# Stick-breaking sums of a two-layer transformer block: the long key rows in two float32r passes, and a place for block one's tables that is given back

## The chip, the core and the metric

The kernel runs on one core of a Trainium2 chip. The metric is device microseconds of one execution. The engines that matter are PE (TensorE, the matmuls), DVE (VectorE), ACT (ScalarE), POOL (GpSimd) and SP, which issues the DMAs. Each engine takes its instructions strictly in the order in which the program lists them, so an instruction that waits holds up all that stand behind it on its engine.

## What is computed

A first block (dilated and windowed attention and an MLP) is followed by two layers of a second block. Each of those layers has a gated feed-forward part, a mixer with three branches (stick-breaking attention, a gated matrix memory, latent attention) and another feed-forward part; there are 512 tokens of width 1024. The change is in the stick-breaking attention, four heads in each layer:

```python
def _stick_breaking_attention(q, k, v):
    """q,k,v: (B,H,S,d). A[t,s] = sigmoid(z_ts) * prod_{s<j<t} (1 - sigmoid(z_tj)), s < t. ..."""
    ...
        z = jnp.einsum('bhqd,bhkd->bhqk', qb, k[:, :, :n], preferred_element_type=jnp.float32) * scale
        ...
        log_keep = jnp.where(mask, jax.nn.log_sigmoid(-z), 0.0)
        ...
        within = jnp.einsum('bhqnj,js->bhqns', lk, tri_in)
        after = jnp.einsum('bhqm,mn->bhqn', jnp.sum(lk, axis=-1), _strict_lower(nk))
        later = (within + after[..., None]).reshape(b, h, Q_BLOCK, n)
        w = jnp.where(mask, jnp.exp(jax.nn.log_sigmoid(z) + later), 0.0)
```

For each query the weight of a key needs the sum of `log_keep` over all later keys up to the query. The sum within a block of 128 keys is a matmul with a triangular matrix; the sum over the later blocks is one row that is carried from block to block.

## The kernel before

**Weights.** `load_w` (L361) brings a weight tile by DMA into `wraw`, casts it on ACT to the upper part `whi` (float32r, L384) and subtracts on DVE to get the lower part `wlo` (L385). Nearly all matmuls are products in three float32r passes (`mm3`). There are two buffers for `wraw` and four each for `whi` and `wlo`: a DMA into `wraw` waits until the `wlo` subtraction of the tile two before it has read that buffer.

**Order.** The order on PE is written out by hand: jobs are generators, `Loom` gives each a due time when it yields a number, and inserts what is due between the weight matmuls; the yields of the stick-breaking heads are `T_SB`, `T_SBR` and `T_SBW` (L1682). On ACT, DVE, POOL and SP a scheduler sets the order when the program is built. `Slots` hands out SBUF places of 4096 bytes per partition (`ND` = 22 of them) and halves of these; a job that needs places yields a condition on `H.room`.

**Stick-breaking.** `sb_job` (L1155) takes the four heads of a layer in two pairs. `stick_scores` (L1428) makes the scores z transposed, keys on partitions, in four key blocks kb: block kb has 512 - 128 kb query columns, so kb 0 to 3 have 512, 384, 256 and 128. Two tiles hold them, one of 1024 columns (kb 0, 1, 3) and one of 256 (kb 2). `stick_head` (L1446) then works on one head: Abs, Exp and Ln on ACT (L1453 to L1455); `sp` and the new z on DVE (L1456, L1457); row 0 of each block is copied to `own` on ACT (L1464), and the diagonal 128 columns are masked on POOL (L1467). After `T_SB` come the four triangular matmuls `sbl<-sbp,trigt` in plain float32, kb 3, 2, 1, 0; between two of them a one-partition DVE add (L1477) puts the sum of the later blocks into row 0 of the next block. At the end DVE subtracts the sums from z (L1480), ACT takes the exponential (L1483), POOL masks the diagonals (L1486), and `sb_job` multiplies by v (`sbo`). The row add is

```python
V.tensor_add(self.tri(sp, kb - 1)[0:1, 128:n + 128], pl[kb][0:1, 0:n], own[kb])
```

**What runs beside it.** Between the stick-breaking steps of a layer's first pair PE multiplies weights (`pt`, six matmuls of 512 columns for one PSUM bank; the bank is read by DVE, `mlv`, L1594) and works on the latent attention (`mla_job`): four transposes `mT` for each head, read from PSUM by ACT into `mhT` (L1358); scores `mls`, reduced by DVE (L1382) and exponentiated by ACT (L1386); transposes `mlT` of the weights `mp`. `carry` and `carryT` are small transposes of the matrix memory's gates, with a chain of one-partition steps on DVE (L1520 to L1527). All these matmuls write one ring of eight PSUM banks, so a matmul also waits until what its bank held before has been read: in the changed program `carry` takes the bank of the first `mT` of the keys, and the first `sbl` of a pair takes the bank that the first `mlv` reads.

Of the kernel before, what the change touches and what calls it, by code (L numbers as in the profile page):

```python
# [155 lines left out]
class Net:  # L156
# [74 lines left out]
    def make_masks(self):  # L231
        nc, C = self.nc, self.const

        self.causal = C.tile([128, S], F32, name="causal")
        nc.vector.memset(self.causal, 0.0)
        own = self.causal[:, 384:512]
        self.sel(own, own, [[-1, 128]], 0, 1, ALU.is_ge, NEG)

        self.band = []
        for name, base in (("band0", 0), ("band1", -1)):  # L240
            m = C.tile([128, 256], F32, name=name)
            nc.vector.tensor_copy(m, self.causal[:, 256:512])
            self.sel(m[:, 0:128], m[:, 0:128], [[1, 128]], base, -1, ALU.is_ge, NEG)
            self.band.append(m)

        self.upper = C.tile([128, 128], F32, name="upper")
        self.sel(self.upper, self.ones, [[1, 128]], -1, -1, ALU.is_ge, 0.0)
        self.upper0 = C.tile([128, 128], F32, name="upper0")
        nc.vector.tensor_copy(self.upper0, self.upper)
        nc.vector.memset(self.upper0[0:1], 0.0)  # L250
        self.trigt = C.tile([128, 128], F32, name="trigt")
        self.sel(self.trigt, self.ones, [[-1, 128]], -1, 1, ALU.is_ge, 0.0)
        nc.vector.memset(self.trigt[0:1], 1.0)
        self.negup = C.tile([128, 128], F32, name="negup")
        nc.vector.memset(self.negup, 0.0)
        self.sel(self.negup, self.negup, [[1, 128]], 0, -1, ALU.is_ge, NEG)
        self.zrow = C.tile([16, 128], F32, name="zrow")
        nc.vector.memset(self.zrow, 0.0)
# [74 lines left out]
    def rope_table(self, name, src, goff, cos, sin, half):  # L333
# [2 lines left out]
        g = self.sc.tile([128, 2 * half], F32, name="rg" + name, tag="rg")  # L336
        nc.sync.dma_start(g, dram(src, goff, [[0, 128], [1, 2 * half]]))
        n = cos.shape[-1] // half
        A = C.tile([128, n, 2 * half], F32, name="rA" + name, tag="rA" + name)
        B = C.tile([128, n, 2 * half], F32, name="rB" + name, tag="rB" + name)  # L340
        cs = cos.rearrange("p (b f) -> p b f", f=half)
        sn = sin.rearrange("p (b f) -> p b f", f=half)
        gl = g[:, 0:half].unsqueeze(1).to_broadcast([128, n, half])
# [207 lines left out]
    def x_tok_job(self, out):  # L551
        for tb in range(TB):
# [212 lines left out]
    def block1(self):  # L765
# [41 lines left out]
        for b in range(TB):  # L807
# [3 lines left out]
        g2, *gains = self.columns("gains", [(a["ln2_g"][0], KB)] + [  # L811
            (a[k][l], KB) for l in range(2) for k in ("ffn1_norm_2", "mix_norm_2", "ffn2_norm_2")], 40.0)
        sinks = self.bcast_row(a["sinks"][0], 8, "sinks")
        self.make_rope()
        self.make_masks()

# [176 lines left out]
            nc.vector.tensor_mul(zt[m // 2][:, m % 2], pg, self.rrow)  # L993
        mix = [zt[i // 2][:, i % 2] for i in range(KB)]
        loom.wait(lambda: not any(left.values()), "units")
        M = T.tile([128, TB, 4], F32, name="dM", bufs=1)
        nc.vector.tensor_max(M, og[0][1][:, :, 0:4], og[1][1][:, :, 0:4])
        nc.vector.tensor_max(M, M, og[2][1][:, :, 0:4])
# [418 lines left out]


    def tri_tiles(self, name):
        return self.H.get(name, [128, 1024]), self.H.get(name + "2", [128, 256])  # L1420

    @staticmethod
    def tri(t, kb):
        o, n = {0: (0, 512), 1: (512, 384), 3: (896, 128), 2: (0, 256)}[kb]
        return t[1 if kb == 2 else 0][:, o:o + n]


    def stick_scores(self, q, k, pr, z):  # L1428

        nc, H = self.nc, self.H  # L1430
        yield lambda: H.room(4096, 4096, 1024, 1024)
        z += [self.tri_tiles("sbz") for _ in range(2)]
        for kbs, i, c0, c1 in ((1, 3), 0, 512, 1024), ((2,), 1, 0, 256), ((0,), 0, 0, 512):
            ps = [self.bank("sbs") for _ in range(2)]
            c = 0
            for kb in kbs:
# [9 lines left out]
    def stick_head(self, z):  # L1446

        nc, H = self.nc, self.H
        V, A, G = nc.vector, nc.scalar, nc.gpsimd
        yield lambda: H.room(4096, 4096, 1024, 1024)  # L1450
        t, sp = self.tri_tiles("sbt"), self.tri_tiles("sbp")
        for i in range(2):
            A.activation(t[i], z[i], AF.Abs)  # L1453
# [8 lines left out]
        for kb in (3, 2, 1, 0):  # L1462
            if kb:
                A.copy(own[kb], self.tri(sp, kb)[0:1])  # L1464
                G.memset(own[kb][:, 0:1], 0.0)
            d = self.tri(sp, kb)[:, 0:128]
            G.tensor_mul(d, d, self.upper0)  # L1467
        yield T_SB
        pl = {1: self.bank("sbl"), 2: self.bank("sbl")}
        pl[3] = pl[1][:, 384:512]  # L1470
        for kb in (3, 2, 1, 0):
            n = S - kb * 128
            if kb == 0:
                pl[0] = self.bank("sbl")
            self.mm(pl[kb][:, 0:n], self.trigt, self.tri(sp, kb), True, True)
            if kb:
                V.tensor_add(self.tri(sp, kb - 1)[0:1, 128:n + 128], pl[kb][0:1, 0:n], own[kb])  # L1477
                yield T_SBR
        for i, c0, c1, kb in ((0, 512, 1024, 1), (1, 0, 256, 2), (0, 0, 512, 0)):
            V.tensor_sub(z[i][:, c0:c1], z[i][:, c0:c1], pl[kb][:, 0:c1 - c0])  # L1480
        H.put(*sp)
        for i in range(2):
            A.activation(z[i], z[i], AF.Exp)  # L1483
        for kb in range(TB):
# [194 lines left out]

T_KD, T_HEADS, T_EXP, T_PT = 22.0, (13.0, 19.0), {1: 4.5, 2: 6.5}, 1.9  # L1680
T_MLA, T_MP, T_MPT = {"q": 12.0, "k": 5.0}, 6.0, 3.5
T_SB, T_SBR, T_SBW = 14.0, 2.5, 3.5  # L1682
T_MS, T_SILU = 3.0, 14.0
CREW = (2, 2, 2)
INS = ["x", "positions", "ln1_g", "w_in", "q_norm_a", "k_norm_a", "q_norm_b", "k_norm_b", "sinks", "w_branch_a",
# [25 lines left out]


ND, SCR = 22, 6
WB = (2, 4)
```

## Time and profile before

| | |
|---|---|
| median of 3 runs | 2324.08 us (2323.95 to 2324.93) |
| the profiled execution | 2323.26 us |
| its span in the profile | 2321.5 us |
| PE busy | 2306.3 us, 99% |
| DVE, ACT, POOL busy | 56%, 39%, 16% |
| the granted TensorE clock | 1.0 in every slice |

The profiled execution lasts 1.8 us longer than its span, so a change of the span is a change of the time. In the rows further down a PE row gives start and modelled duration; matmuls overlap, so what one costs is the distance to the start of the next. "x4" merges four instructions in a row.

### The profile page before, as it was taken

Reading aid. Unit: us, or ns where it says so; the run is one execution under the profiler, and the core shown is the slowest. Engines: PE = TensorE matmul, PEld = TensorE weight load, DVE = VectorE, ACT = ScalarE, POOL = GpSimd, SP = SyncE. Lnnn points to the kernel's source line nnn. Section 1 sums busy time; section 2 is a strip of 40 time slices with the busy share of each in tenths; the row PEclk is TensorE's granted clock in tenths of the full one; section 3 lists DMA queues with packets and bytes.
Section 4 is the critical chain, followed back from the end, with each engine's and each line's share of the span. In section 5 each row is a group of like instructions: output and inputs, shape, how many; then the busy total and the mean of one; then the engine's idle time right before and its main releaser. Section 6 shows DMA issues by size and latency. Waiting matters only on the chain.

```text
span 2321.5 us, 28445 instructions
## 1 busy us (share of the span) xinstructions
PE 2306.3 (99%) x10884; PEld 1902.3 (82%) x10884; DVE 1294.5 (56%) x2255; ACT 914.9 (39%) x1517; POOL 381.4 (16%) x385
## 2 busy tenths in 40 slices
PE   8999999999999999999999999999999999999999
PEld 7888888888888888877888888888888778888887
DVE  7844556444355445678564555455457674646552
ACT  7655432222223323656533333223236673333331
POOL 2000023101022112111111311211211101213110
PEclk9999999999999999999999999999999999999999
DMA  4223333233323323313323333333233142323332
GB/s 139 65 64 92 100 100 99 85 105 95 98 87 105 100 92 96 97 55 91 105 63 91 109 91 91 100 92 100 91 102 91 46 114 73 89 83 105 92 100 87
DMA packets 250525, 213.68 MB, mean 92 GB/s; under 512 B 14231, under 2 KB 234133, under 8 KB 250389
## 3 DMA queue, kind: packets, MB, share of 16 engines
q1 hardware_dynamic: 250388, 211.87, 30.8%
q8 instruction: 85, 1.39, 0.2%
q14 instruction: 52, 0.42, 0.1%
HBM read 208.64 MB, written 3.19 MB: 91 GB/s over the span
## 4 chain that ended last, share of the span: by engine, by line
PE 96%; ACT 1%; DVE 1%; DMA 1%; SPq 0%; issue 0%; ACTq 0%
PE pgate L205 15%; PE pd L205 15%; PE pt L205 13%; PE pg L205 10%; PE pa L205 10%; PE pu L205 8%; PE pf L205 6%; PE po L205 6%; PE pbr L205 5%; PE mls L205 1%; PE mnum L205 1%; PE sbl L205 1%; PE mss L205 1%; PE dio L205 1%; PE s L205 1%; PE pT L212 0%
## 5 line engine op out<-in xcount | busy, mean ns | idle before, releaser
L385 DVE TENSOR_TENSOR wlo<-wraw,whi 128x1024 fp32r<-128x1024 f32 (+3 forms) x394 | 550.6, 1398 | 412.3 <-ACT whi L384 407.4
L384 ACT CAST whi<-wraw 128x1024 fp32r<-128x1024 f32 (+3 forms) x394 | 404.6, 1027 | 649.7 <-PE pg L205 141.6
L205 PE MATMUL pd<-hidh,whi 128*128 128x512 f32 x520 | 202.3, 389 | 0.0
L205 PE MATMUL pd<-hidl,whi 128*128 128x512 f32 x520 | 202.3, 389 | 0.0
L205 PE MATMUL pd<-hidh,wlo 128*128 128x512 f32 x520 | 202.3, 389 | 0.0
L205 PE MATMUL pgate<-xh,whi 128*128 128x512 f32 x512 | 201.3, 393 | 0.0
L205 PE MATMUL pgate<-xh,wlo 128*128 128x512 f32 x512 | 199.4, 389 | 0.0
L205 PE MATMUL pgate<-xl,whi 128*128 128x512 f32 x512 | 199.2, 389 | 0.0
L205 PE MATMUL pt<-whi,xl 128*128 128x512 f32 (+2 forms) x480 | 172.1, 358 | 0.0
L205 PE MATMUL pt<-whi,xh 128*128 128x512 f32 (+2 forms) x384 | 140.4, 366 | 0.1
L205 PE MATMUL pa<-xl,whi 128*128 128x512 f32 x352 | 137.2, 390 | 0.8 <-DVE xl L476 0.7
L205 PE MATMUL pa<-xh,whi 128*128 128x512 f32 x352 | 137.6, 391 | 0.0
L205 PE MATMUL pg<-xh,whi 128*128 128x512 f32 x352 | 137.4, 390 | 0.0
L205 PE MATMUL pa<-xh,wlo 128*128 128x512 f32 x352 | 137.1, 389 | 0.0
L205 PE MATMUL pg<-xh,wlo 128*128 128x512 f32 x352 | 137.0, 389 | 0.0
L205 PE MATMUL pg<-xl,whi 128*128 128x512 f32 x352 | 137.0, 389 | 0.0
L205 PE MATMUL pt<-wlo,xh 128*128 128x512 f32 (+2 forms) x384 | 134.1, 349 | 0.0
L587 POOL TENSOR_TENSOR t<-t,t 128x512 f32<-128x512 f32 x44 | 56.8, 1290 | 426.6 <-ACT whi L384 313.4
L205 PEld LDWEIGHTS pd<-hidl,whi 128*128 128x128 f32 x520 | 97.6, 188 | 20.4
L205 PEld LDWEIGHTS pd<-hidh,whi 128*128 128x128 f32 x520 | 97.6, 188 | 20.3
L205 PEld LDWEIGHTS pd<-hidh,wlo 128*128 128x128 f32 x520 | 97.6, 188 | 20.1
L205 PEld LDWEIGHTS pt<-whi,xl 128*128 128x128 f32 x480 | 102.5, 214 | 12.6
(524 smaller groups left out, 4674.0 us busy)
## 6 DMA issues: line engine op xcount, KB each, us to landing
wraw<-in_w_in_dram SPq DMA_DIRECT2D x116, 512.0 KB
wraw<-in_ffn_wi_dram SPq DMA_DIRECT2D x176, 256.0 KB
wraw<-in_ffn_wo_dram SPq DMA_DIRECT2D x34, 512.0 KB
wraw<-in_w_up_dram SPq DMA_DIRECT2D x32, 512.0 KB
wraw<-in_w_out_dram SPq DMA_DIRECT2D x24, 512.0 KB
wraw<-in_w_down_dram SPq DMA_DIRECT2D x24, 512.0 KB
wraw<-in_w_in_dram SPq DMA_DIRECT2D x32, 256.0 KB
wraw<-in_ffn_wo_dram SPq DMA_DIRECT2D x12, 384.0 KB
```

Source lines behind the costliest of these rows:

```text
L205: self.nc.tensor.matmul(out, lhsT, rhs, start=start, stop=stop)
L384: nc.scalar.copy(hi, raw)
L385: nc.vector.tensor_sub(lo, raw, hi.bitcast(F32))
L587: nc.gpsimd.tensor_mul(t2, t2, t1)
```

## The change

The matmuls of kb 1 and kb 0 take their input in two float32r parts: `split_to` casts the 896 columns of both blocks on ACT into `sph` and subtracts on DVE into `spl`, and `trigr`, the triangular matrix as float32r, multiplies both into one bank. kb 3 and kb 2 stay in plain float32 and share a tile of 384 columns. The row that is carried into kb 1 and kb 0 is now added into `own`, and `row_split` puts its upper and lower parts into row 0 of `sph` and `spl` (a cast and a subtraction on DVE, on one partition). The scores come in the order (2, 3), 1, 0. The band masks and the rope tables of block one move into a `Slots` place `k1` that is put back after block one; `ND` becomes 23, and the conditions for places grow. The core of the diff:

```diff
-            m = C.tile([128, 256], F32, name=name)
+            m = self.k1[:, len(self.band) * 256:len(self.band) * 256 + 256]
...
-        self.trigt = C.tile([128, 128], F32, name="trigt")
-        self.sel(self.trigt, self.ones, [[-1, 128]], -1, 1, ALU.is_ge, 0.0)
-        nc.vector.memset(self.trigt[0:1], 1.0)
+        tri = self.scr("tri")[:, 0:128]
+        self.sel(tri, self.ones, [[-1, 128]], -1, 1, ALU.is_ge, 0.0)
+        nc.vector.memset(tri[0:1], 1.0)
+        self.trigr = C.tile([128, 128], F32R, name="trigr")
+        nc.vector.tensor_copy(self.trigr, tri)
+        self.trigt = self.trigr.bitcast(F32)
...
+    def row_split(self, hi, lo, t):
+        V = self.nc.vector
+        V.tensor_copy(hi, t)
+        V.tensor_sub(lo, t, hi.bitcast(F32))
...
+        self.k1 = H.get("k1", [128, 1024])
...
+        H.put(self.k1)
...
-        return self.H.get(name, [128, 1024]), self.H.get(name + "2", [128, 256])
+        return self.H.get(name, [128, 896]), self.H.get(name + "2", [128, 384])
 
     @staticmethod
     def tri(t, kb):
-        o, n = {0: (0, 512), 1: (512, 384), 3: (896, 128), 2: (0, 256)}[kb]
-        return t[1 if kb == 2 else 0][:, o:o + n]
+        i, o, n = ((0, 0, 512), (0, 512, 384), (1, 0, 256), (0, 896, 128) if t[0].shape[1] == 1024 else (1, 256, 128))[kb]
+        return t[i][:, o:o + n]
...
-        yield lambda: H.room(4096, 4096, 1024, 1024)
+        yield lambda: H.room(4096, 4096, 1536, 1536)
         z += [self.tri_tiles("sbz") for _ in range(2)]
-        for kbs, i, c0, c1 in ((1, 3), 0, 512, 1024), ((2,), 1, 0, 256), ((0,), 0, 0, 512):
+        for kbs, i, c0, c1 in ((2, 3), 1, 0, 384), ((1,), 0, 512, 896), ((0,), 0, 0, 512):
...
-        yield lambda: H.room(4096, 4096, 1024, 1024)
+        yield lambda: H.room(4096, 4096, 4096, 1536, 1536)
...
+        two = [H.get(n, [128, 896], F32R) for n in ("sph", "spl")]
+        self.split_to(*two, sp[0])
+        H.put(sp[0])
         yield T_SB
-        pl = {1: self.bank("sbl"), 2: self.bank("sbl")}
-        pl[3] = pl[1][:, 384:512]
+        pl = {2: self.bank("sbl")}
+        pl[3] = pl[2][:, 256:384]
         for kb in (3, 2, 1, 0):
             n = S - kb * 128
-            if kb == 0:
-                pl[0] = self.bank("sbl")
-            self.mm(pl[kb][:, 0:n], self.trigt, self.tri(sp, kb), True, True)
-            if kb:
-                V.tensor_add(self.tri(sp, kb - 1)[0:1, 128:n + 128], pl[kb][0:1, 0:n], own[kb])
-                yield T_SBR
-        for i, c0, c1, kb in ((0, 512, 1024, 1), (1, 0, 256, 2), (0, 0, 512, 0)):
+            if kb < 2:
+                pl[kb] = self.bank("sbl")
+                for i in range(2):
+                    self.mm(pl[kb][:, 0:n], self.trigr, self.tri(two[i:], kb), i == 0, i == 1)
+            else:
+                self.mm(pl[kb][:, 0:n], self.trigt, self.tri(sp, kb), True, True)
+            if kb == 3:
+                V.tensor_add(self.tri(sp, 2)[0:1, 128:n + 128], pl[kb][0:1, 0:n], own[kb])
+                yield T_SBR[0]
+            elif kb:
+                V.tensor_add(own[kb], pl[kb][0:1, 0:n], own[kb])
+                self.row_split(*(self.tri(two[i:], kb - 1)[0:1, 128:n + 128] for i in range(2)), own[kb])
+                yield T_SBR[1]
+        for i, c0, c1, kb in ((1, 0, 384, 2), (0, 512, 896, 1), (0, 0, 512, 0)):
             V.tensor_sub(z[i][:, c0:c1], z[i][:, c0:c1], pl[kb][:, 0:c1 - c0])
-        H.put(*sp)
+        H.put(sp[1], *two)
...
-T_SB, T_SBR, T_SBW = 14.0, 2.5, 3.5
+T_SB, T_SBR, T_SBW = 14.0, (2.5, 3.2), 3.5
...
-ND, SCR = 22, 6
+ND, SCR = 23, 6
```

On PE the rows stand as before except for the first parts of the stick-breaking work: in a layer's first pair all four `mls` of 128 columns now stand ahead of the two `sbl` of 128, two `mlT` stand between the `sbl` of the two heads' kb 1, and the four `mls` of 256 columns stand ahead of the `sbl` of kb 0 instead of behind it. In the second pair the `sbl` steps are spread further apart. On ACT and DVE more has moved. The places below are in the first layer's first pair; the second layer has the same order.

On ACT, around the copies of the latent attention's key transposes (`mhT<-mT,hgk`), before:

```order
L1455 ACTIVATE sbt2_7885<-sbt2_7885 128x256
L1358 ACTIVATE mhT_7969<-mT_7970,hgk_7148 96x512
L1464 COPY own_7922<-sbp_7910 1x128
L1464 COPY own_7923<-sbp_7910 1x384
L1464 COPY own_7922<-sbp2_7911 1x256
L1358 ACTIVATE mhT_7969<-mT_7982,hgk_7148 96x512
L384 CAST whi_8139<-wraw_8138 128x1024
L1358 ACTIVATE mhT_8000<-mT_8001,hgk_7148 96x512
L384 CAST whi_8312<-wraw_8311 128x1024
L1358 ACTIVATE mhT_8000<-mT_8013,hgk_7148 96x512
L384 CAST whi_8399<-wraw_8398 128x1024
```

and after, where `sph_7917` and `sph_7946` are the casts of the two heads:

```order
L1479 COPY own_7934<-sbp2_7923 1x256
L576 CAST sph_7917<-sbp_7894 128x896
L1479 COPY own_7935<-sbp_7922 1x384
L1373 ACTIVATE mhT_7974<-mT_7975,hgk_7145 96x512
L576 CAST sph_7946<-sbp_7922 128x896
L1373 ACTIVATE mhT_7974<-mT_7987,hgk_7145 96x512
L1373 ACTIVATE mhT_8005<-mT_8006,hgk_7145 96x512
L391 CAST whi_8276<-wraw_8275 128x1024
L1373 ACTIVATE mhT_8005<-mT_8018,hgk_7145 96x512
L391 CAST whi_8416<-wraw_8415 128x1024
```

The first head's cast now stands ahead of all four `mhT` copies and the second head's ahead of the last three; before, the first `mhT` copy came right behind the last Ln.

On DVE, ahead of the gate chain (`carry`), before:

```order
L1457 SCALAR_TENSOR_TENSOR sbz_7808<-sbz_7808,sbt_7909 128x1024
L1457 SCALAR_TENSOR_TENSOR sbz2_7807<-sbz2_7807,sbt2_7885 128x256
L385 TENSOR_TENSOR wlo_8140<-wraw_8138,whi_8139 128x1024
L1520 COPY carry_8022<-carry_8019 1x16
L1521 COPY carry_8022<-carry_8019 1x16
L1526 TENSOR_TENSOR carry_8022<-carry_8022 1x12
L385 TENSOR_TENSOR wlo_8313<-wraw_8311,whi_8312 128x1024
```

and after:

```order
L1472 SCALAR_TENSOR_TENSOR sbz_7805<-sbz_7805,sbt_7921 128x896
L577 TENSOR_TENSOR spl_7918<-sbp_7894,sph_7917 128x896
L392 TENSOR_TENSOR wlo_8147<-wraw_8145,whi_8146 128x1024
L577 TENSOR_TENSOR spl_7947<-sbp_7922,sph_7946 128x896
L1546 COPY carry_8027<-carry_8024 1x16
L1547 COPY carry_8027<-carry_8024 1x16
L1552 TENSOR_TENSOR carry_8027<-carry_8027 1x12
L392 TENSOR_TENSOR wlo_8277<-wraw_8275,whi_8276 128x1024
```

The two subtractions `spl` stand on both sides of the first `wlo`. Further along on DVE, at the first copy of a `pt` bank (`mlv`), before:

```order
L1524 TENSOR_TENSOR carry_8022<-carry_8022 1x4
L1525 TENSOR_TENSOR carry_8022<-carry_8022 1x4
L1594 SCALAR_TENSOR_TENSOR mlv_7791<-pt_7799,rcy_7216,br_mv_7789 128x4x128
L1382 ISA mp_8061,mlm_8062<-mls_8064,causal_440 128x128
L1382 ISA mlm_8062 128x1
L1382 ISA mp_8061,mlm_8062<-mls_8070,causal_440 128x128
```

and after:

```order
L1550 TENSOR_TENSOR carry_8027<-carry_8027 1x4
L1551 TENSOR_TENSOR carry_8027<-carry_8027 1x4
L392 TENSOR_TENSOR wlo_8417<-wraw_8415,whi_8416 128x1024
L1620 SCALAR_TENSOR_TENSOR mlv_7788<-pt_7796,rcy_7213,br_mv_7786 128x4x128
L1397 ISA mp_8066,mlm_8067<-mls_8069,causal_437 128x128
L1397 ISA mlm_8067 128x1
```

A third weight subtraction, `wlo_8417`, now stands ahead of `mlv` and of the reductions of the scores; before, it stood behind them all.

On ACT at the end of the pair, where `sbz` are the exponentials of the heads and `ysb` copies the product with v, before:

```order
L1483 ACTIVATE sbz_7806<-sbz_7806 128x1024
L1483 ACTIVATE sbz_7808<-sbz_7808 128x1024
L1386 ACTIVATE mp_8061,mld_8211<-mp_8061,mnm_8215 128x256
L1386 ACTIVATE mp_8061,mld_8211<-mp_8061,mnm_8221 128x256
L1386 ACTIVATE mp_8088,mld_8228<-mp_8088,mnm_8232 128x256
L1386 ACTIVATE mp_8088,mld_8228<-mp_8088,mnm_8238 128x256
L384 CAST whi_8549<-wraw_8548 128x1024
L1177 COPY ysb_8267<-sbo_8258 128x512
```

and after:

```order
L1401 ACTIVATE mp_8085,mld_8214<-mp_8085,mnm_8224 128x256
L1509 ACTIVATE sbz_7803<-sbz_7803 128x896
L1509 ACTIVATE sbz2_7804<-sbz2_7804 128x384
L391 CAST whi_8552<-wraw_8551 128x1024
L1509 ACTIVATE sbz_7805<-sbz_7805 128x896
L1192 COPY ysb_8296<-sbo_8287 128x512
```

A weight cast, `whi_8552`, now stands between the exponentials of the two heads; before, it stood behind both.

## Rows read from the trace of the kernel before

**Rows 1.** The page: busy time of each engine; the chain that ended last, by engine.
```profile
PE 2306.3 (99%) x10884; PEld 1902.3 (82%) x10884; DVE 1294.5 (56%) x2255; ACT 914.9 (39%) x1517; POOL 381.4 (16%) x385
...
PE 96%; ACT 1%; DVE 1%; DMA 1%; SPq 0%; issue 0%; ACTq 0%
```

**Rows 2.** Waits of PE, longest first: for what, total us, times, longest.
```profile
PE colT L212 <- DMA rows<-in_ln_g_dram: 5.0, 1, 5.0
```

**Rows 3.** Tile sbl: duration ns min/median/max, first and last start us, forms.
```profile
L205 PE MATMUL sbl<-sbp,trigt x56: 271/483/594, 996.0 to 1879.4; 128*128 128x128 f32 x16, 128*128 128x384 f32 x16, 128*128 128x512 f32 x16, 128*128 128x256 f32 x8
```

**Rows 4.** Timeline of PE, first layer: start us, duration us, instruction.
```profile
967.85 0.28 PE L205 MATMUL pt<-whi,xh 128*128 128x256 f32 x1
967.97 0.28 PE L205 MATMUL pt<-wlo,xh 128*128 128x256 f32 x1
...
993.28 0.39 PE L205 MATMUL pt<-whi,xl 128*128 128x512 f32 x1
993.51 0.39 PE L205 MATMUL pt<-whi,xh 128*128 128x512 f32 x1
...
1003.46 1.46 PE L205 MATMUL sbl<-sbp,trigt 128*128 128x384 f32 x4
1004.85 0.24 PE L212 MATMUL carryT<-ident,carry 1*16 1x1 f32 x4
...
1007.18 1.88 PE L205 MATMUL sbl<-sbp,trigt 128*128 128x512 f32 x4
1008.90 1.89 PE L205 MATMUL mls<-mhT 96*128 96x256 f32 x8
```

**Rows 5.** The page's costliest groups: a weight load, count, busy us and mean ns.
```profile
L205 PEld LDWEIGHTS pd<-hidl,whi 128*128 128x128 f32 x520 | 97.6, 188 | 20.4
```

**Rows 6.** Timeline of PE where the new waits would stand.
```profile
991.21 0.17 PE L212 MATMUL carry<-ident,rowF 16*1 16x16 f32 x1
...
995.55 0.61 PE L205 MATMUL mls<-mhT 96*128 96x128 f32 x4
995.99 0.61 PE L205 MATMUL sbl<-sbp,trigt 128*128 128x128 f32 x4
...
1013.45 2.37 PE L205 MATMUL sbo<-sbz,sbv 128*64 128x512 f32 x16
```

**Rows 7.** Timeline of ACT, first layer, with idle time before and what ended it.
```profile
987.51 0.41 ACT L1455 ACTIVATE sbt<-sbt 128x256 f32<-128x256 f32 x1
987.83 0.67 ACT L1358 ACTIVATE mhT<-mT,hgk 96x512 f32<-96x512 f32 x1
...
996.99 1.05 ACT L384 CAST whi<-wraw 128x1024 fp32r<-128x1024 f32 x1 [3.61 <-DMA wraw<-in_w_in_dram]
...
1009.16 2.26 ACT L1483 ACTIVATE sbz<-sbz 128x1024 f32<-128x1024 f32 x2 [1.48 <-DVE sbz L1480]
```

**Rows 8.** Timeline of DVE, first layer.
```profile
984.83 1.23 DVE L1456 SCALAR_TENSOR_TENSOR sbp<-sbz,sbt 128x1024 f32<-128x1024 f32 x1 [0.98 <-ACT sbt L1455]
...
991.32 1.40 DVE L385 TENSOR_TENSOR wlo<-wraw,whi 128x1024 fp32r<-128x1024 f32 x1
...
995.75 0.75 DVE L1594 SCALAR_TENSOR_TENSOR mlv<-pt,rcy,br_mv 128x512 f32<-128x512 f32 x1 [0.19 <-PE pt L205]
...
1005.48 1.00 DVE L1477 TENSOR_TENSOR sbp<-sbl,own 1x384 f32<-1x384 f32 x2
```

**Rows 9.** Timeline of POOL, first layer: masks of the diagonals.
```profile
986.13 1.50 POOL L1467 TENSOR_TENSOR sbp<-sbp,upper 128x128 f32<-128x128 f32 x1 [5.12 <-DVE sbp L1456]
...
993.04 0.45 POOL L1467 TENSOR_TENSOR sbp<-sbp,upper 128x128 f32<-128x128 f32 x1
```

**Rows 10.** Timeline of SP: issues of weight DMAs.
```profile
992.75 2.22 SPq L382 DMA_DIRECT2D wraw<-in_w_in_dram  x2
```

**Rows 11.** Second layer, timeline of DVE: the weight subtraction that frees the buffer.
```profile
1784.70 1.38 DVE L385 TENSOR_TENSOR wlo<-wraw,whi 128x1024 fp32r<-128x1024 f32 x1
```

**Rows 12.** Second layer, timeline of ACT: the cast of that next weight tile.
```profile
1789.68 1.05 ACT L384 CAST whi<-wraw 128x1024 fp32r<-128x1024 f32 x1 [2.92 <-PE mls L205]
```

More of the change, by code (lines that the diff above doesn't have):

```diff
@@ L338, in rope_table @@
         n = cos.shape[-1] // half
-        A = C.tile([128, n, 2 * half], F32, name="rA" + name, tag="rA" + name)
-        B = C.tile([128, n, 2 * half], F32, name="rB" + name, tag="rB" + name)
+        if name in ("qa", "ka"):
+            o = 512 if name == "qa" else 768
+            A, B = (self.k1[:, c:c + 128].rearrange("p (n f) -> p n f", f=2 * half) for c in (o, o + 128))
+        else:
+            A = C.tile([128, n, 2 * half], F32, name="rA" + name, tag="rA" + name)
+            B = C.tile([128, n, 2 * half], F32, name="rB" + name, tag="rB" + name)
         cs = cos.rearrange("p (b f) -> p b f", f=half)
@@ L1467, in stick_head @@
             G.tensor_mul(d, d, self.upper0)
+        two = [H.get(n, [128, 896], F32R) for n in ("sph", "spl")]
+        self.split_to(*two, sp[0])
+        H.put(sp[0])
         yield T_SB
-        pl = {1: self.bank("sbl"), 2: self.bank("sbl")}
-        pl[3] = pl[1][:, 384:512]
+        pl = {2: self.bank("sbl")}
+        pl[3] = pl[2][:, 256:384]
         for kb in (3, 2, 1, 0):
             n = S - kb * 128
-            if kb == 0:
-                pl[0] = self.bank("sbl")
-            self.mm(pl[kb][:, 0:n], self.trigt, self.tri(sp, kb), True, True)
-            if kb:
-                V.tensor_add(self.tri(sp, kb - 1)[0:1, 128:n + 128], pl[kb][0:1, 0:n], own[kb])
-                yield T_SBR
-        for i, c0, c1, kb in ((0, 512, 1024, 1), (1, 0, 256, 2), (0, 0, 512, 0)):
+            if kb < 2:
+                pl[kb] = self.bank("sbl")
+                for i in range(2):
+                    self.mm(pl[kb][:, 0:n], self.trigr, self.tri(two[i:], kb), i == 0, i == 1)
+            else:
+                self.mm(pl[kb][:, 0:n], self.trigt, self.tri(sp, kb), True, True)
[7 more added lines that the diff above has]
+        for i, c0, c1, kb in ((1, 0, 384, 2), (0, 512, 896, 1), (0, 0, 512, 0)):
             V.tensor_sub(z[i][:, c0:c1], z[i][:, c0:c1], pl[kb][:, 0:c1 - c0])
-        H.put(*sp)
+        H.put(sp[1], *two)
         for i in range(2):
```

## The prediction

> **What bounds the kernel now.** I read the page first. PE is busy for 2306.3 of 2321.5 us, and 96% of the chain that ended last is PE [rows 1]. Of the 15.2 us in which PE is idle, the waits view puts the longest single one, 5.0 us, on a load at the start of the program [rows 2]; it names no wait in a mixer. So two things move the time: PE work that goes away, one for one, and any wait that is put in PE's way. The other engines have slack only until somebody on PE waits for them, and the timelines of the first layer's first pair [rows 6 to 10] show where that is near. PE's order is written by hand and nearly kept, so a late operand isn't stepped around: PE stands still.
>
> **What PE is relieved of.** The tile view counts sixteen float32 passes each of 384 and 512 columns [rows 3], that is eight matmuls of each in two passes, one for every head. The cost is taken from start to start [rows 4]: four passes of 384 take 1004.85 - 1003.46 = 1.39 us, 0.695 for a matmul, and four of 512 take 1008.90 - 1007.18 = 1.72 us, 0.86 for a matmul. A float32r pass of 512 columns takes 993.51 - 993.28 = 0.23 us and one of 256 takes 0.12; between them 384 columns are 0.175. Two passes then cost 0.35 and 0.46 us. A head saves 0.345 + 0.40 = 0.745 us, and eight heads save **6.0 us**.
>
> Each new pass brings a weight load, and a load lasts 188 ns [rows 5], longer than the 0.12 us from one pass of 256 columns to the next: loads are hidden here even with one for each pass. The Trainium skill says otherwise (TensorE: Matmul & The Clock Gate, the mechanism in the part on packing small matmuls): loads overlap matmuls in flight only where their row groups differ. The trace contradicts that with the distances of 0.12 and 0.23 us; by that rule the change would save nothing on PE, the last rival below.
>
> The other edits of PE's order only permute rows, and the constants and the place `k1` belong to the program's start: I cost them at nothing, since DVE and POOL write the same numbers of elements there, but for one copy of 128 columns.
>
> **What is added, and who waits for it.** For each head ACT casts 896 columns, DVE subtracts 896, and four short DVE operations prepare the rows. This is off PE, but in front of things that PE needs. I place the changed order by hand on the clock of the trace before, for the first layer's first pair. There are four places.
>
> (a) *carry.* In the old order the last Ln ends at 987.92 and the first `mhT` follows at once [rows 7]. In the new order the two large Ln come last; with the same elements in sum they end near 987.0 and 987.8. DVE then makes sp of both heads (1.23 us for 1024 columns [rows 8], so 1.1 for 896), the first at 988.1. POOL masks three diagonals before the first head's cast may start. A mask takes 0.45 us at best and 1.50 beside DVE work [rows 9]; three of them end between 990.0 and 992.3. DVE runs sp and z through 991.1, so I take 991.3, near the contended price. The cast (1.05 for 1024 columns [rows 7], 0.9 here), a short copy of row 0 and `mhT` (0.67 [rows 7]; the copy I take as half of it) follow, to 993.2. PE stands at `carry` from 991.21 on [rows 6], because that takes the bank which `mhT` reads: **2.0 us** of standing, 0.7 to 3.0.
>
> The masks slow down beside DVE as the two ends 0.45 and 1.50 show. The Trainium skill has a reason (GPSIMD Engine Reference, key points): GpSimd shares its SBUF interfaces with VectorE and contends with DVE instructions of two SBUF inputs, which sp and z are. This rule speaks against the change, since the masks now gate a cast on ACT; at the uncontended price (a) would be 0.7 us and not 2.0.
>
> (b) *The first sbl.* Behind the cast, DVE subtracts `spl` (1.1 us), to 993.3, and only then the weight part `wlo` (1.3 by [rows 8]), to 994.6. That frees the buffer for the next weight DMA. In the old order the issue stood at 992.75 [rows 10] and the cast that waited for it came at 996.99 [rows 7], 4.2 us later; in the second layer it was at most 3.6 us (issue at the end of `wlo`, 1786.08 [rows 11], cast at 1789.68, where PE was the last to be waited for [rows 12]). With 4.2 the cast starts at 998.8, ends at 999.85, the third `wlo` ends at 1001.05, and behind it `mlv` (0.75 [rows 8]) ends at 1001.8. PE would reach the first `sbl`, which takes the bank of `mlv`, at 996.4, behind two `mls` more than before (995.99 and another 0.44 [rows 6]). It is **5.4 us** late in all, (a) included; 4.8 in the second layer. With the ends of (a) and of the DMA this is 3.5 to 6.4. In the old order nothing stood there: `mlv` waited for PE, not PE for it [rows 8].
>
> (c) *After the sbl of kb 1.* Two row adds of 384 columns take 1.00 us [rows 8]; two casts and two subtractions of such rows are new, each between nothing and the price of an add, 0.5, so up to 2.0 us. Behind them stand the copy of `carryT`, whose bank the fourth `mls` of 256 columns takes, and the first reduction of these `mls`, whose bank the next `pt` takes. Placed in the same way these two come 0 to 2.3 us late, by the price of a row operation; I take **1.2**.
>
> (d) *sbo.* The cast `whi_8552` waits for the last reader of its buffer on PE, and the second head's exponential stands behind it. From that matmul's end: cast 1.05 [rows 7], exponential of 896 columns 1.0 (2.26 for two of 1024 [rows 7]), a mask 0.45 to 1.4 [rows 9] make 2.5 to 3.45 us. PE has six `pt` of 0.23 in that time, 1.4 us, ahead of `sbo`, where it stood at 1013.45 without a wait [rows 6]. **1.4 us** of 1.1 to 2.1.
>
> In the second pair the steps lie 12 to 25 weight matmuls apart, 2.7 to 5.7 us, against 0.5 us for a row add alone, or 1.5 for an add, a cast and a subtraction and 1.3 for a `wlo` between them; I take 0 and keep 1.0 a layer as the upper end, since other DVE work stands there too. What hides the rest of the added ACT and DVE work is PE's weight matmuls; where that cover ends, it is in (a) to (d).
>
> **Sum.** First layer 5.4 + 1.2 + 1.4 = 8.0 us, second layer 4.8 + 1.2 + 1.4 = 7.4 us: 15.4 us of waits against 6.0 us saved, +9.4. The profiled execution would go from 2323.26 to 2332.7; the median of the runs lies 0.8 us above it, so 2324.1 + 9.4 = **2333 us**, rounded down. The ends: at least 3.5 + 0 + 1.1 = 4.6 in a layer, +3.2 in sum, 2327; at most 6.4 + 2.3 + 2.1 + 1.0 = 11.8, +17.6, 2342.
>
> **Rivals.** *All covered.* The saving is real and PE waits for nothing: 2324.1 - 6.0 = 2318, faster. This needs (a) to (d) below 0.7 us in a layer, the point from which the gain could be measured. The place is the ring of banks: (a), (b) and the second half of (c) hold only if `carry`, the first `sbl` and `pt` get the banks that I read for them, and if those banks are read as late as I place it. For it speaks that the waits view before knows no such wait in the same ring [rows 2]; against it that cast, subtraction, DMA, cast, subtraction and `mlv` stand in one row, and that even their lower ends leave 3.5 us. *Even.* The lower ends hold (masks uncontended, the transfer at 3.6, row operations at the price of a copy): 3 to 5 us a layer, against 3.0 saved, gives 2324 to 2328. For it speaks that each end has a row. *No saving.* If the load of each float32r pass were not hidden, two passes of 384 columns would cost 2 x (0.188 + 0.175) = 0.73 us and two of 512 2 x (0.188 + 0.23) = 0.84, as much as the float32 ones; the waits alone would count, 2324 + 15 = 2339. The distances in [rows 4] are against it.
>
> **How the numbers follow.** About 0.2%, 4.65 us, is what a measurement of this kernel can tell from no change: faster is below 2319.4, slower above 2328.7. The forecast family, waits of 5.3 us a layer and more, has 0.60; no saving 0.03; even 0.27; all covered 0.10. So slower 0.63, same 0.27, faster 0.10. The range leaves out the covered case and the top corner where all upper ends meet: 2321 to 2340.
>
> **What would show it.** Right: the waits view of after lists PE `carry` on ACT `mhT`, PE `sbl` on DVE `mlv`, `mls` or `pt` on a DVE row operation or reduction, and `sbo` on POOL, once in each layer, and PE's idle time grows by some 15 us while its busy time falls by about 6. The cast `sph` on ACT shows idle time that POOL ended, and `whi` in front of the third `wlo` idle time that a DMA ended. Wrong: PE idle stays near 15 us (all covered), or float32r passes of 384 columns lie 0.35 us apart (no saving), or a wait stands at a place that I cost at nothing, the second pair or the product with v there.

## The result

| | before | after |
|---|---|---|
| median of the runs | 2324.01 us (2322.43 to 2324.93, 6 runs) | 2337.29 us (2336.12 to 2339.00, 6 runs) |
| the profiled execution, its span | 2323.26, 2321.5 us | 2338.72, 2337.0 us |

The ratio is 1.006, with a 95% interval of 1.005 to 1.0071: the change costs 13.3 us. The forecast was 2333, the range 2321 to 2340. The page of after, as [rows 1] of before (busy time, then the chain that ended last):

```profile
PE 2309.2 (99%) x10884; PEld 1906.4 (82%) x10884; DVE 1312.2 (56%) x2296; ACT 920.3 (39%) x1525; POOL 388.0 (17%) x385
...
PE 92%; DVE 3%; ACT 3%; DMA 1%; issue 1%; POOL 1%; SPq 0%; ACTq 0%; POOLq 0%
```

PE is idle for 27.8 us, 12.6 more than before, and DVE, ACT and POOL have come into the chain. That PE's busy time did not fall by 6 but rose by 2.9 us is the first sign of something unforeseen. The waits of PE in after, as [rows 2] (what was waited for, total us, times, longest):

```profile
PE carry L212 <- ACT mhT L1373: 6.2, 2, 3.5
...
PE pt L205 <- DVE mlm L1397: 2.3, 2, 1.1
PE sbl L205 <- DVE mlv L1620: 1.9, 2, 1.2
PE sbo L205 <- POOL sbz L1512: 1.4, 2, 0.7
```

Four waits are new, each twice, once in either layer. Here they are on PE's timeline, beside [rows 4, 6] (start, modelled duration, idle before and what ended it); the last two rows are the second layer's:

```profile
994.93 0.17 PE L212 MATMUL carry<-ident,rowF 16*1 16x16 f32 x1 [2.72 <-ACT mhT L1373]
...
996.33 0.63 PE L205 MATMUL pt<-wlo,xh 128*128 128x512 f32 x1
996.75 0.63 PE L205 MATMUL pt<-whi,xl 128*128 128x512 f32 x1
...
1000.89 1.05 PE L205 MATMUL mls<-mhT 96*128 96x128 f32 x8
1003.10 0.46 PE L205 MATMUL sbl<-sbt,trigr 128*128 128x128 f32 x2 [1.16 <-DVE mlv L1620]
...
1011.38 2.40 PE L205 MATMUL mls<-mhT 96*128 96x256 f32 x8
1014.92 0.50 PE L205 MATMUL pt<-whi,xh 128*128 128x512 f32 x1 [1.14 <-DVE mlm L1397]
1016.41 0.39 PE L205 MATMUL sbl<-sph,trigr 128*128 128x512 f32 x1
...
1021.51 1.07 PE L205 MATMUL sbo<-sbz,sbv 128*64 128x512 f32 x2
1023.30 2.37 PE L205 MATMUL sbo<-sbz,sbv 128*64 128x512 f32 x14 [0.72 <-POOL sbz L1512]
1025.59 0.92 PE L205 MATMUL sbs<-sbq,sbk 64*128 64x256 f32 x8
...
1795.47 0.18 PE L212 MATMUL carry<-ident,rowF 16*1 16x16 f32 x1 [3.49 <-ACT mhT L1373]
...
1802.48 1.05 PE L205 MATMUL mls<-mhT 96*128 96x128 f32 x8
```

In before, first layer, what stands behind the `mls` of 256 columns and behind the `sbo` group starts here:

```profile
1010.44 0.58 PE L205 MATMUL pt<-whi,xh 128*128 128x512 f32 x1
...
1015.75 1.14 PE L205 MATMUL sbs<-sbq,sbk 64*128 64x384 f32 x8
```

Two `pt` passes lie 0.42 us apart behind the wait of `carry`, against 0.23 in [rows 4]. The windows view says why (busy time of each engine, then PEclk, the granted clock); first layer, then second layer:

```profile
990.00:995.00 5.00, 2.28 (x16) 1.71 (x14) 3.68 (x5) 2.56 (x6) 4.44 (x10) 1.00 0.00 0
995.00:1000.00 5.00, 5.00 (x17) 3.92 (x18) 4.24 (x12) 3.64 (x6) 0.32 (x1) 0.66 0.34 105
...
1790.00:1795.00 5.00, 1.98 (x12) 1.41 (x10) 3.69 (x4) 2.69 (x7) 4.45 (x10) 0.95 0.00 0
1795.00:1800.00 5.00, 4.53 (x12) 3.56 (x13) 4.26 (x7) 4.03 (x6) 0.86 (x1) 0.50 0.35 105
1800.00:1805.00 5.00, 4.29 (x23) 3.54 (x22) 3.82 (x21) 1.37 (x3) 0.00 (x0) 0.87 0.42 114
```

After PE has stood still for 2.72 and 3.49 us the clock is at the lower of its two levels (0.50, 1.2 GHz) for some microseconds, and PE counts as busy for longer with the same work. So the loss has a fifth part that no wait shows. Measured from start to start on PE, with before in brackets:

| us | first layer | second layer |
|---|---|---|
| wait at `carry` | 2.72 (0) | 3.49 (0) |
| `carry` to the first `mls`, 18 passes between | 5.96 (4.34) | 7.01 (4.34) |
| wait at the first `sbl` | 1.16 (0) | 0.71 (0) |
| the `mls` of 256 columns, to the next instruction | 3.54 (1.54) | 3.54 (1.54) |
| the `sbo` group, to the next instruction | 4.08 (2.30) | 4.08 (2.30) |
| lost | 9.28 | 10.65 |

That is 19.9 us. Less the forecast saving of 6.0 it is 13.9, against 13.3 in the medians. In the span the difference is 15.5, since the profiled run of after lies 1.4 us above its median and that of before 0.8 below; 0.6 of it is a wait of `sbl` for a row add further on, 0.9 is there before the first wait, and the kernel **consts** below has nearly the same (its `carry` starts at 992.05, before's at 991.21) without being slower.

### The profile page after: what moved, and what is told of

The parts are those of the page before. It is cut to its first block, busy times and chain, and to the rows that moved or that the text cites. A ratio compares the mean times of both kernels' runs of the same rounds, so it can differ in the third digit from the quotient of the medians.

```text
span 2337.0 us, 28485 instructions
## 1 busy us (share of the span) xinstructions
PE 2309.2 (99%) x10884; PEld 1906.4 (82%) x10884; DVE 1312.2 (56%) x2296; ACT 920.3 (39%) x1525; POOL 388.0 (17%) x385
## 4 chain that ended last, share of the span: by engine, by line
PE 92%; DVE 3%; ACT 3%; DMA 1%; issue 1%; POOL 1%; SPq 0%; ACTq 0%; POOLq 0%
PE pgate L205 15%; PE pd L205 15%; PE pt L205 11%; PE pg L205 10%; PE pa L205 10%; PE pu L205 7%; PE po L205 6%; PE pbr L205 5%; PE pf L205 5%; PE mnum L205 1%; DMA wraw<-in_w_in_dram 1%; PE mss L205 1%; ACT whi L391 1%; PE mls L205 1%; PE dio L205 1%
```

## The experiments

Theory at the start: the waits come from a chain of cast, subtraction and weight steps in front of four instructions. Rivals: the lower clock is part of the new work itself, the new tiling costs time on PE, or the memory part does. The kernels below are compared with runs of before on the same chip.

**nosplit: PE's work of after without the split.** Both passes multiply the sums as they are; cast, subtraction and row split are left out.

```diff
-        two = [H.get(n, [128, 896], F32R) for n in ("sph", "spl")]
-        self.split_to(*two, sp[0])
-        H.put(sp[0])
...
+        two = [sp[0], sp[0]]
...
-                self.row_split(*(self.tri(two[i:], kb - 1)[0:1, 128:n + 128] for i in range(2)), own[kb])
```

> The changed kernel with PE's order kept row for row, but without the splits: sp of kb 1 and kb 0 is written as float32r at once and both passes multiply it, so the casts, the subtractions and the row splits are left out, and the values of these sums are not the reference's. Theory (waits from the order on ACT and DVE; the two passes save 6.0 us): no wait at carry, the clock stays at 1.0; the first sbl still waits for mlv about 2.5 us, because the third weight subtraction still stands ahead of it; sbo still loses 1.8 us, since the weight cast still stands between the exponentials; about 4.6 us a layer against 3.0 saved, so 2326 to 2328. Rival A (the split work alone costs the time): everything gone, 2318. Rival B (float32r passes save nothing, as PE's busy time rose from 2306 to 2309 us): 2330 to 2333.

Measured: 2330.72 us, ratio 1.0029 (1.0018 to 1.0041). That is 6.8 us above before, about half of the 13.3; with the saving of 6.0 us added to both, 12.8 of 19.3 us of loss need no split. By the time alone this is rival B, no saving. The parts speak against it: `sbl` waits 6.6 us, the `sbo` groups take 3.77 us each against 2.30, 2.9 more in both layers, and behind its second-layer wait of 3.56 us the clock was at 0.50, which the expectation did not have: from that `sbl` to the one of 256 columns it is 5.68 us, against 3.28 in the first layer, 2.4 more. That is 11.9, less 6.0 makes 5.9 of the 6.8; ns_tie5 below settles it. The waits, then PE and DVE in the first layer:

```profile
PE sbl L205 <- DVE mlv L1621: 6.6, 2, 3.6
...
PE sbo L205 <- POOL sbz L1513: 0.8, 2, 0.4
```
```profile
1000.22 0.46 PE L205 MATMUL sbl<-sbt,trigr 128*128 128x128 f32 x2 [3.02 <-DVE mlv L1621]
```
```profile
998.19 1.23 DVE L392 TENSOR_TENSOR wlo<-wraw,whi 128x1024 fp32r<-128x1024 f32 x1 [1.70 <-ACT whi L391]
999.33 0.74 DVE L1621 SCALAR_TENSOR_TENSOR mlv<-pt,rcy,br_mv 128x512 f32<-128x512 f32 x1
```

`carry` and `pt` wait no more, so these two belong to the split. `sbl` still waits, for `mlv`, and `mlv` stands behind the third `wlo`, which waits for a cast that waited 3.35 us for its weight DMA. Here the scheduler's order is enough.

**late: the split issued behind the pause `T_SB`,** so that the casts fall behind the first `mhT` copies.

```diff
-        self.split_to(*two, sp[0])
-        H.put(sp[0])
         yield T_SB
+        self.split_to(*two, sp[0])
+        H.put(sp[0])
```

> The changed kernel with the cast and the subtraction of both heads issued behind the yield T_SB instead of ahead of it, nothing else. On ACT both casts then stand behind the first two copies of the keys' transposes. Theory: the wait at carry (2.7 and 3.5 us) goes, and with it the half clock behind it; the wait for mlv stays at about 3 us, and the later ones at 2.0 and 1.8 us: some 7 us a layer against 3.0 saved, 2331 to 2333. Rival (the chain over the weight DMA sets the end whatever stands at carry): no gain, 2337.

Measured: 2339.24 us, 1.0063 (1.0048 to 1.0078), no better than after.

```profile
PE sbl L205 <- DVE mlv L1620: 5.4, 2, 2.7
...
PE mls L205 <- ACT mhT L1373: 3.4, 2, 1.8
PE pt L205 <- DVE mlm L1397: 2.3, 2, 1.1
PE sbo L205 <- POOL sbz L1512: 1.4, 2, 0.7
```

The wait of `carry` is gone, 6.2 us, and two others, one of them new at an `mls`, hold 6.9 more: the steps stand in one row, and it matters little where PE meets it. The expectation that this edit would gain fell, the rival held.

**pool: late, with the cast behind the last `mhT` and the subtraction on GpSimd.**

```diff
+        cast = A.copy(two[0], sp[0])
+        self.after(cast, self.mhk)
+        G.tensor_sub(two[1], sp[0], two[0].bitcast(F32))
```

> As late, but the casts are tied behind the last copy of the keys' transposes, and the subtraction of the lower part runs on POOL instead of DVE. Theory: as nosplit at carry and mlv (0 and 2.5 us a layer), the waits behind the row splits stay (2.0), sbo 1.8: 6.3 a layer against 3.0 saved, 2330 to 2331. Rival (POOL's subtraction comes too late for the sbl of kb 1): a new wait of PE on POOL spl of 1 to 3 us a layer, 2333 to 2336.

Measured: 2345.18 us, 1.0092 (1.0077 to 1.0107), the worst of all; `sbl` waits 10.4 us for `mlv` and 3.2 for a row add. A plain miss of theory and rival; what the next kernel shows on DVE is here too, two gate additions of 1.95 and 2.00 us (996.26 and 998.24) beside GpSimd's subtractions, and behind them the third `wlo` ahead of `mlv`.

**rows_pool: pool, with the third `wlo` tied behind the first row add, the row splits on GpSimd and `T_SBW` 5.0.**

> As pool, and three more edits, one for each wait that is left: the third weight subtraction behind the row add is tied behind it, the row splits run on POOL, and T_SBW is 5.0 instead of 3.5, so that sbo comes later on PE. Theory: all four waits go but for some 0.5 us a layer, and the 6.0 us are left: 2318 to 2320, faster than both. Rival (POOL as the new late one): waits of PE on POOL at the sbl of kb 1 or kb 0 of 1 to 2 us a layer, 2321 to 2324.

Measured: 2330.11 us, 1.0027 (1.0017 to 1.0038), above theory and rival both. The waits of `pt` and `sbo` are gone and `carry` has 0.2 left, but `sbl` waits for `mlv` by 4.37 and 4.38 us, though no `wlo` is in front. DVE, then POOL, first layer:

```profile
995.69 0.15 DVE L1563 TENSOR_TENSOR carry<-carry 1x4 f32<-1x4 f32 x1
...
995.87 1.93 DVE L1562 TENSOR_TENSOR carry<-carry 1x4 f32<-1x4 f32 x1
997.84 2.00 DVE L1563 TENSOR_TENSOR carry<-carry 1x4 f32<-1x4 f32 x1
999.87 0.15 DVE L1562 TENSOR_TENSOR carry<-carry 1x4 f32<-1x4 f32 x1
```
```profile
995.70 4.12 POOL L1497 TENSOR_TENSOR spl<-sbp,sph 128x896 fp32r<-128x896 f32 x2
```

Two additions of four numbers take 2 us each instead of 0.15, for exactly as long as GpSimd's two subtractions run. The way round is the one of [rows 9], only in the other direction: there a mask on POOL took 1.50 instead of 0.45 us beside DVE work.

**ns_tie: nosplit with one order added,** the third `wlo` behind the first row addition.

```diff
+                if self.due == 0:
+                    self.after(lw, self.radd)
```

> The kernel of nosplit (both one-pass products read the sums as they are: no cast, no subtraction, no row split, so the lower parts are left out of the computation) with one order added: the third weight subtraction of the layer stands behind the first row addition, not ahead of the mixer's output step (mlv). Theory: in nosplit the whole 6.6 us of waiting of sbl for mlv came from that subtraction (it waits 1.70 us for a weight cast that waits for its DMA) and from the slower clock after it; with it out of the way mlv runs at about 996.5 and sbl waits under 0.3 us per layer. Then TensorE's saving of 6.0 us shows alone: 2318 us (2317 to 2320). Rival: the four score products now ahead of sbl make it wait for mlv in any order (the bank is handed on later): 2322 to 2326, with a wait sbl <- mlv of 1 to 2 us per layer.

Measured: 2321.26 us, 0.9989 (0.998 to 0.9999), 2.1 us below its before where nosplit lies 6.8 above: 8.9 us by one order. `sbl` waits 0.6 us in both layers together, so the theory on `mlv` holds, but the time is 3 us above it. The rest is in `sbo`: 3.77 us a layer from its start to the next instruction, against 2.30 before. ACT has the weight cast between the two exponentials, as the forecast said for (d), also without any split:

```profile
1012.92 1.06 ACT L392 CAST whi<-wraw 128x1024 fp32r<-128x1024 f32 x1 [1.44 <-PE pt L206]
1013.88 0.95 ACT L1516 ACTIVATE sbz<-sbz 128x896 f32<-128x896 f32 x1
```

**ns_tie5: ns_tie with `T_SBW` 5.0 instead of 3.5.**

> The kernel of ns_tie (lower parts left out of the computation, third weight subtraction behind the row addition) with the pause ahead of the output products (sbo) 5.0 in place of 3.5. Theory: of the 5.9 us per execution that TensorE is spared in ns_tie (per layer 1.22 us on the four pairs of one-pass products of pair 1, as much on those of pair 2, and 0.5 us on the transposes beside them), 2.9 us went into sbo, which holds TensorE for 3.77 us a layer in place of 2.30 because the second exponential stands behind a weight cast. With sbo one group of weight products later this is gone: sbo 2.3 us, and 2318.3 us (2317.5 to 2319.5). Rival: the price of sbo comes from the new tiling of the sums (896 and 384 columns) and not from when it starts: sbo stays near 3.8 us and the time near 2321.

Measured: 2317.2 us, 0.9972 (0.996 to 0.9983). Of the new waits only 0.3 us at one `sbl` is left, `sbo` takes 2.30 us again, and before's time less 6.2 us remains. This is the saving by itself.

**consts: before with the tables of block one in the place that is given back and `ND` 23, and nothing else.**

> The kernel before with the part of the change that touches the stick-breaking sums left out: only the masks and tables of block one in a place that is given back, and one buffer more of the pool. Theory: the memory part carries no time of its own: 2324 us, within 0.1 %, with the waits of the kernel before. Rival: the start, 0.9 us later in the changed kernel when it reaches the first mixer's key tiles, comes from here: 2325 us.

Measured: 2323.37 us, 0.9997 (0.9988 to 1.0006). The memory part costs nothing, and 0.84 us at the first `carry` says nothing of the time.

**delay: before, with idle copies on ScalarE ahead of the first key tile.** Nothing of the change is in it.

```diff
+                if n == "k" and h == 0:
...
+                    for _ in range(1 + 3 * self.layer):
+                        dm = A.copy(idle, self.causal)
```

> The kernel before, with idle copies of 128x512 on ScalarE ahead of the first key tile (mhT): one in the first mixer, four in the second; the four key tiles keep their order. Nothing of the change is in it. Theory: the clock falls because TensorE stands still for some 3 us, whatever it stands still for. The first mixer's wait of carry for mhT is 0.5 to 1.5 us and its clock stays at 1.00; the second's is 3 to 4 us and is followed by some microseconds at 0.50, as in the changed kernel. Time 2329 to 2333 us: waits of 4 to 5.5 and 2 to 4 us for the slow stretch. Rival: the low clock comes with the change's own work (the new one-pass products, or the casts beside them): the clock stays at 1.00 in both mixers and the time is 2327 to 2329, the waits alone.

Measured: 2332.23 us, 1.0038 (1.0024 to 1.0051). The waits are 2.7 us at `carry` in the second layer, and 2.68 and 0.79 at an `mls` behind `mlv`. PE behind the one in the first layer:

```profile
998.75 0.71 PE L205 MATMUL mls<-mhT 96*128 96x128 f32 x4 [2.68 <-DVE mlv L1601]
...
999.99 0.63 PE L205 MATMUL pt<-whi,xh 128*128 128x512 f32 x1
1000.41 0.63 PE L205 MATMUL pt<-wlo,xh 128*128 128x512 f32 x1
```
```profile
1000.00:1005.00 5.00, 5.00 (x17) 4.02 (x16) 3.19 (x14) 0.97 (x5) 0.00 (x0) 0.66 0.23 77
```

The same fall, to 0.50, with 0.42 us between passes, in a program that has no new pass and none of the change's casts: the fall needs no part of the change. It comes behind a PE that has stood still, though not behind every such wait: nosplit's 3.02 us in the first layer were followed by 1.00. I had expected it in the second layer only; the delay made a long wait in the first one too, at another place than I named. The time is in the expected range, by other parts than expected: waits of 6.2 us and two slow stretches.

**spl_dve: the whole computation, with the added steps elsewhere.** Cast behind the last `mhT`, subtraction on VectorE behind the first row add, third `wlo` behind it too, row splits on GpSimd, `T_SBW` 5.0.

```diff
+                self.after(V.tensor_sub(two[1], sp[0], two[0].bitcast(F32)), self.radd)
```

> The full computation of the changed kernel, with its added steps put elsewhere: the cast of the upper part on ScalarE behind the last key tile (mhT), the subtraction of the lower part (128x896) on VectorE behind the first row addition, not ahead of mlv; the third weight subtraction behind the row addition too; the two-instruction row splits on GpSimd; the weight loads' spacing 5.0 in place of 3.5. Theory: the change's loss is only a matter of what stands ahead of four instructions on ScalarE, VectorE and GpSimd; with nothing big ahead of mhT, mlv, the score reductions and the exponentials, the waits carry <- mhT, sbl <- mlv, pt <- mlm and sbo <- sbz are each under 0.5 us, no stretch runs at the lower clock, and the saving of 6.0 us remains: 2318 to 2321 us. Rival: the two subtractions (1.0 us each) only move the wait on to the next user of VectorE, the transposes of the probabilities (mlT) or the one-pass products: 2322 to 2326 with a new wait of 1 to 2.5 us per layer there.

Measured: 2326.02 us, 1.0012 (1.0002 to 1.0021). `carry` and `sbo` are free (0.7 us in both layers for `sbo`), `sbl` waits 0.2 for `mlv`. In their place `pt` waits 3.1 us for the score reductions and `sbl` 1.8 for the rows from GpSimd: the rival. One reason is again on two engines at once, a gate step of 16x128 numbers on DVE, 0.27 us in after, here beside the row splits on POOL:

```profile
1007.99 1.07 DVE L1573 TENSOR_TENSOR rowm<-rowg,rowF 16x128 f32<-16x128 f32 x1
```
```profile
1007.87 1.04 POOL L578 TENSOR_TENSOR spl<-own,sph 1x384 fp32r<-1x384 f32 x1
```

A third loss is in the clock. PE waits at `pt` for the same 1.54 us in both layers, and only in the second the clock falls behind it, to 0.50: up to the eleventh matmul from there it is 3.99 us (1804.43 to 1808.42), against 2.43 in the first layer.

```profile
1009.91 0.50 PE L206 MATMUL pt<-whi,xh 128*128 128x512 f32 x1 [1.54 <-DVE mlm L1405]
...
1804.43 0.66 PE L206 MATMUL pt<-whi,xh 128*128 128x512 f32 x1 [1.54 <-DVE mlm L1405]
```

**best3: nothing of the split on GpSimd, the lower part in two pieces.** 384 columns behind the first row add, 512 behind the row split of kb 2, the first of a head's two (the expectation calls it the second); the row splits' casts are on ScalarE; more time ahead of the one-pass products, the gates' transposes and `sbo`.

```diff
-T_SB, T_SBR, T_SBW = 14.0, (2.5, 3.2), 3.5
+T_SB, T_SBR, T_SBW = 14.0, (2.5, 4.5), 6.0
...
+                self.after(part(slice(512, 896)), self.radd)
...
+                    self.after(part(slice(0, 512)), rs)
...
-        yield 12.0
+        yield 16.0
         p4 = self.bank("carryT")
```

> The full computation. As spl_dve (cast of the upper part behind the last key tile, third weight subtraction behind the row addition), with the lower part's subtraction in two pieces on VectorE: 128x384 behind the first row addition, 128x512 behind the second row split; the row splits' casts on ScalarE and their subtractions on VectorE, so none of it on GpSimd; pauses: 4.5 ahead of the one-pass products (3.2 before), 16 ahead of the carries' transposes (12), 6.0 ahead of the output products (3.5). Theory: each part of the change has a place where it costs nothing, and the saving of 5.9 us on TensorE is then left: carry, sbl, pt and sbo wait under 0.5 us each per layer, the granted clock is 1.00 throughout, 2318 to 2320 us. Rival: VectorE is too full between the first and the last of these products for two more microseconds in any order; a wait of 1 to 2 us per layer comes back at the one-pass products or at the score products, and the time is 2322 to 2326.

Measured: 2319.43 us, 0.9982 (0.9973 to 0.9992): with the whole computation, below after and, by a little, below before. Its waits in the mixers and the passes of kb 1:

```profile
PE pt L206 <- DVE mlm L1405: 1.3, 2, 0.7
...
PE sbl L206 <- DVE mlv L1635: 0.6, 2, 0.3
```
```profile
1005.58 0.34 PE L206 MATMUL sbl<-sph,trigr 128*128 128x384 f32 x1
1005.75 0.34 PE L206 MATMUL sbl<-spl,trigr 128*128 128x384 f32 x1
1005.93 0.34 PE L206 MATMUL sbl<-sph,trigr 128*128 128x384 f32 x1
```

The clock is 1.00 throughout. What is left of the loss is mostly at the `mls` of 256 columns, 2.61 us against 1.54 in each layer.

**best4: best3 with `T_SBW` 4.0.**

> As best3 with the pause ahead of the output products 4.0 in place of 6.0, which puts them one group of weight products earlier. Theory: the same 2318 to 2320 us, since the exponentials are done by then in either order. Rival: sbo waits 0.5 to 1.5 us a layer for the second exponential, as in the changed kernel, and the time is 1 to 3 us above best3.

Measured: 2319.46 us, 0.9984 (0.9975 to 0.9993), the same: once the exponentials are done, it does not matter when `sbo` comes.

## Why the forecast held, and where its sizes were off

**The saving, forecast 6.0 us: right.** ns_tie5 is 6.2 us faster than before, and passes of 384 columns lie 0.17 to 0.18 us apart (best3), where the estimate was 0.175. The loads, 188 ns each, are hidden. In after the transposes `mlT` stand between these passes, and there two of them cost 0.44 us and not 0.35. So the sum is right by some luck: in ns_tie5 the groups of kb 1 (with the transposes) and kb 0 of a layer's first pair take 1.41 and 0.94 us, against 2.24 and 1.72 before, 1.6 less, and those of the second pair about 1.3 less, where the forecast had 1.5 for each. The rival "no saving" is out. So is the sign by which I wanted to see the saving, a fall of PE's busy time by 6: at the lower clock the same work counts as busy for longer. Where the clock stays at 1.00 the sign is there: PE of ns_tie5 is busy for 2300.6 us, 5.7 less than before.

**(a) `carry`, forecast 2.0 us: the place right, the size too small.** Measured 2.72 and 3.49, the second outside the 0.7 to 3.0. The chain is the forecast one: ACT's cast waits for POOL and `mhT` stands behind it. The three masks gating the first cast, POOL and then ACT:

```profile
989.14 2.51 POOL L1482 TENSOR_TENSOR sbp<-sbp,upper 128x128 f32<-128x128 f32 x2 [5.93 <-DVE sbp L1471]
...
991.64 1.26 POOL L1482 TENSOR_TENSOR sbp<-sbp,upper 128x128 f32<-128x128 f32 x1
```
```profile
992.94 0.94 ACT L576 CAST sph<-sbp 128x896 fp32r<-128x896 f32 x1 [2.31 <-POOL own L1480]
...
994.20 0.67 ACT L1373 ACTIVATE mhT<-mT,hgk 96x512 f32<-96x512 f32 x1
```

All three cost 1.26 us; the fourth, at 992.90 with DVE idle, cost 0.45. So in the first layer the end lay at the upper end of the term, not below it, and taking an end between the two prices was the error of this step. Here the trace agrees with the Trainium skill (GPSIMD Engine Reference, the specifications), which has GpSimd and VectorE contend for their SBUF interfaces where a DVE instruction has two inputs in SBUF, as sp and z have. By the rows a mask takes 2.8 times as long beside them. In the second layer the way from the first mask to `carry` is the same, 5.79 us, but PE is there 0.8 us earlier.

**(b) the first `sbl`, forecast 5.4 and 4.8 us with (a): the sum right in the first layer, its make-up not.** I had 2.0 at `carry` and the rest at `mlv`. Measured are 2.72 + 1.16 of waits and 1.62 of slower passes, 5.5 us, in the first layer, and 3.49 + 0.71 + 2.67 = 6.9 in the second. The clock is the step that the forecast lacks: it had no term for it. In the first layer the slow passes took the place of a wait that would have stood at `sbl` anyway, since there a DMA ended the wait of the cast ahead of the third `wlo`; in the second they were on top, for there that cast waited for PE (ACT, second layer):

```profile
1801.13 1.05 ACT L391 CAST whi<-wraw 128x1024 fp32r<-128x1024 f32 x1 [1.62 <-PE pt L205]
```

The order half of (b), the third `wlo` ahead of `mlv`, is shown by nosplit against ns_tie; the split's half by `carry`, which waits 6.2 us in after and not at all in nosplit. The issue of the DMA to the cast took 3.5 us here (996.47 to 999.98) where I took 4.2, and the `wlo` ahead of it ended some 0.9 us later than I placed it; the two nearly cancel, so the first layer's sum is in part luck.

**(c) after kb 1, forecast 1.2 us: 2.0 in each layer.** Inside the range of 0 to 2.3, and by the forecast row: two adds of 0.55, two casts of 0.34 and two subtractions of 0.54 us on one partition. What I left out of the working are the gates' steps `rowg`, `rowd`, `rowm`, 1.0 us from 1013.47 to 1014.45, which stand on DVE between `carryT`'s copy and the first reduction. nosplit has the same gates' steps, but with the first reduction ahead of them and no row split, and no such wait; with the row splits on GpSimd 0.3 us a layer are left (rows_pool).

**(d) `sbo`, forecast 1.4 us: 1.78 in each layer.** The cast at 1020.26 and the second exponential at 1021.21 are the forecast ones. It is a matter of order and of `T_SBW`, for the most part not of the split: 1.47 of the 1.78 us are there without any split (ns_tie), and none with `T_SBW` 5.0 (ns_tie5).

**The second pair, forecast 0 to 1.0 us: right.** The waits view names one 0.6 us there at most, `sbl` on a row add.

Put together: 8.0 + 7.4 us of losses were forecast and 9.3 + 10.6 were found; of the 4.5 us between, 2.1 are (b) in the second layer, where the clock costs 2.67, 1.6 are (c) and 0.8 are (d). The time lies inside the range because the range kept room for upper ends that did not all come; the clock, 4.3 us of slower passes in after, was no part of it. The rival "all covered" describes ns_tie5, so it was a fair rival, but of another order of the same instructions.

## What to carry to other kernels

Where one engine is 99% busy and its order is fixed, count an edit's gain only after each moved instruction on the slower engines has been placed against the next thing that the busy engine wants; here one order and one pause made 6.8 us above before into 6.2 below with the same matmuls (nosplit, ns_tie5). A wait on PE may cost a second time in the clock behind it, 1.6 to 2.7 us here; its length alone does not tell whether it will, so price a wait with and without this. Elementwise work moved to GpSimd to relieve VectorE can slow VectorE by more than it takes away: in pool two subtractions of 1.1 us left VectorE, and two of its additions grew by 1.8 us each.

## What the runs showed of the hardware that I had not expected

- The granted clock went from 1.00 to 0.50 with waits of 2.68, 2.70, 2.72 and 3.49 us (delay, after), of 3.56 us (nosplit, second layer) and of only 1.54 us (spl_dve, second layer). It stayed at 1.00 behind 1.54 us in spl_dve's first layer and behind 3.02 us in nosplit's. So the length of the wait by itself does not decide; what else does, these runs do not settle. A slow stretch lasted some 3.4 us behind the 2.72, and 18 passes then took 5.96 us instead of 4.34.
- One-partition DVE additions of four numbers took 1.93 and 2.00 us in rows_pool and 1.95 and 2.00 in pool, not 0.15, beside a two-input subtraction of 128x896 on GpSimd.
- Two float32r passes of 384 columns cost 0.44 us between transposes (after) and 0.35 among themselves (best3).
